# Products of attention probabilities with V: two heads alternating between the column halves of TensorE

## The chip, the cores and the metric

One Trainium2 chip, one core. The metric is the device time of one execution in microseconds (us), as the median of several executions. The profile is one execution, seen by the hardware profiler.

## What is computed

A block of two layers over 512 latent tokens and 256 context tokens, 1024 wide. Each layer runs three token mixers side by side (a recurrence, a full attention, an attention in a window of 128 tokens), merges them with gates, and ends in a mixture of experts. What matters here is the attention. Both kinds have 8 query heads of 64 elements and 2 heads of keys and values, so four query heads share one V. Cut from the reference:

```python
def attend(q, keys, vals):                      # full attention
    qg = q.reshape(q.shape[0], q.shape[1], ATT_KV, group, HEAD_DIM)
    logits = jnp.einsum('bqhgd,bkhd->bhgqk', qg, keys).astype(jnp.float32) * ATTN_SCALE
    p = jax.nn.softmax(logits, axis=-1).astype(vals.dtype)
    o = jnp.einsum('bhgqk,bkhd->bqhgd', p, vals)
```

The windowed kind sees the 256 context keys and up to three tiles of 128 latent keys, and has one more logit per head, a sink. Context queries see context keys alone. All is float32. In the second layer only latent queries are needed.

## The kernel before, in words

Tokens lie in 6 tiles of 128: tiles 0 and 1 are context, 2 to 5 latent. `attention` (L707) makes, for each of the two branches, a unit for keys and values (`attn_kv`, L774) and one unit of queries for each head of keys (`attn_q`, L809), and then calls `attend_unit` (L814) four times per layer: two branches, two heads of keys.

`attend_unit` walks over items: every query tile, and in it four heads. Layer 0 has 6 tiles, so 24 items in a unit; layer 1 has 4 tiles, so 16. Item i passes through stages in successive steps of one loop:

- step i: `attend_qk` (L846) makes the scores S in PSUM (two float32r passes, L876; masks L878), VectorE the row maximum (L883, or L885 and L886), ScalarE the exponential into P with the row sum (L888), VectorE the reciprocal and the scaling of P (L892, L893).
- step i + 2: `attend_t` (L896) transposes P on TensorE in blocks of 128 keys (L904), and ScalarE copies the blocks into a tile PT (L905).
- step i + 3: `attend_pv` (L908) multiplies: for each block of keys one float32 matmul with V (64 columns) as the stationary operand and the block of PT (128 queries) as the moving one (L915). The 64 outputs of a head land in partitions 0 to 63 for an even head and 64 to 127 for an odd one, which are the two halves of the array's columns; heads 0 and 1 share one column block of the accumulator `oT`, heads 2 and 3 the other. After head 3 ScalarE copies the accumulator to `os` (L919) and POOL's queue stores it (L920). `oT` has one buffer.

A head has 2, 4, 5 or 6 blocks of keys. A float32 matmul stands in the trace as two records, each with its own weight load, so a head leaves 4, 8, 10 or 12 records on L915.

After the scores and after the transposes of each step the loop calls `F.fill(fu)`: it issues other work of about `fu` microseconds by the author's own estimate (0.6 to 1.0): gate projections (`gate`, L930; matmuls L503), products of the modulation (`mod`, L277; L286) which go round four quarters of the array's columns, and in some units the projections (L245 to L247) and the key preparation of the next branch. What the fills leave over is issued after the attention. The engines' final order is set when the program is built: a scheduler sorts by priority, which is the order of the code, and by what it estimates to be ready, so neighbours can change places. Semaphores are put in from the use of buffers: a tile of a tag with n buffers waits for the release of the n-th tile before it.

Key preparation (L795 to L806): for each of 6 tiles, ScalarE writes the rounded keys twice into a tile `ks` (L799), VectorE the rests (L801), TensorE transposes four blocks (L805), ScalarE copies them to `kT` (L806). `ks` and PT have two buffers each before the change; P has three.

Of the kernel before, what the change touches and what calls it, by code (L numbers as in the profile page):

```python
# [9 lines left out]
F32 = mybir.dt.float32  # L10
F32R = mybir.dt.float32r
# [12 lines left out]
NT = T // 128  # L24
# [102 lines left out]
class Block:  # L127
# [646 lines left out]
    def attn_kv(self, L, br, p, kv):  # L774
        nc = self.nc
        c0 = COL_ATT[br]
        gk = None
        kv["sink"] = kv["gq"] = None
        if br == 0:
            gq = p.tile([128, 64], F32, name="gq", tag="gq")  # L780
            gk = p.tile([128, 64], F32, name="gk", tag="gk")
            self.bcast(gq, self.I["attn_q_norm_g"][L])
            self.bcast(gk, self.I["attn_k_norm_g"][L])
            nc.vector.tensor_scalar(gq, gq, 0.125, None, op0=OP.mult)
            kv["gq"] = gq
        else:
            sink = p.tile([128, 8], F32, name="sink", tag="sink")
            self.bcast(sink, self.I["swa_sink"][L])
            kv["sink"] = sink
        V = kv["V"] = self.pre.pop(1) if self.pre else p.tile([128, NT, 128], F32, name="aV", tag="aV", bufs=2)  # L790
        w = self.w_split(self.w_load(self.win(L, c0 + 512, 256)))
        yield from self.attn_unit(L, br, p, w, list(range(NT)), 2, gk, 1.0, V)
        raw = self.raw
        kT = kv["kT"] = p.tile([128, 2, 2, T], F32R, name="kT", tag="kT", bufs=2)
        for t in range(NT):  # L795
            ks = p.tile([128, 2, 2, 2, 64], F32R, name="ks", tag="ks", bufs=2)
            hv = raw[:, t, :128].rearrange("p (h d) -> p h d", d=64)
            for d in range(2):
                nc.scalar.activation(ks[:, :, 0, d], hv, AF.Copy)  # L799
            for d in range(2):  # L800
                nc.vector.tensor_tensor(ks[:, :, 1, d], hv, ks.bitcast(F32)[:, :, 0, d], op=OP.subtract)  # L801
            b = self.ps.tile([128, 4, 128], F32R, name="ktp", tag="tp")
            for j in range(2):
                for s in range(2):
                    nc.tensor.transpose(b[:, 2 * j + s, :], ks[:, j, s].rearrange("p a d -> p (a d)"), self.idr[:, :128])  # L805
            nc.scalar.activation(kT[:, :, :, t * 128:(t + 1) * 128].rearrange("p j s t -> p (j s) t"), b, AF.Copy)  # L806
            yield 0.25
# [6 lines left out]
    def attend_unit(self, L, br, p, j, kv, fu):  # L814
        F = self.F
        items = [(t, hh) for t in self.ot for hh in range(4)]
        n = len(items)
        st = {}
        qT = {self.ot[0]: self.attend_q(p, j, self.ot[0], kv)}
        for i in range(n + 3):  # L820
            if i < n:
                t, hh = items[i]
                st[i] = self.attend_qk(L, br, p, j, items[i], kv, qT[t])
                if hh == 1 and i + 3 < n:
                    qT[t + 1] = self.attend_q(p, j, t + 1, kv)
                F.fill(fu)
            if 0 <= i - 2 < n:
                self.attend_t(p, st[i - 2])
                F.fill(fu)
            if 0 <= i - 3 < n:  # L830
                self.attend_pv(L, br, p, j, st.pop(i - 3), kv)

    def attend_q(self, p, j, t, kv):
        nc = self.nc
# [61 lines left out]
    def attend_t(self, p, st):  # L896
        nc = self.nc
        t, hh, kt, P, _ = st
        PT = p.tile([128, NT, 128], F32, name="PT", tag="PT", bufs=2)
        for a in range(0, len(kt), 4):  # L900
            e = min(a + 4, len(kt))
            b = self.ps.tile([128, 4, 128], F32, name="ptp", tag="tp")
            for i in range(a, e):
                nc.tensor.transpose(b[:, i - a, :], P[:, i * 128:(i + 1) * 128], self.ident)  # L904
            nc.scalar.activation(PT[:, a:e], b[:, :e - a], AF.Copy)  # L905
        st[4] = PT

    def attend_pv(self, L, br, p, j, st, kv):  # L908
        nc = self.nc
        t, hh, kt, P, PT = st  # L910
        if hh == 0:
            self.oacc = self.ps.tile([128, 2, 128], F32, name="oT", tag="acc", bufs=1)
        q = slice(64 * (hh % 2), 64 * (hh % 2) + 64)
        for i, k in enumerate(kt):
            nc.tensor.matmul(self.oacc[q, hh // 2, :], kv["V"][:, k, j * 64:(j + 1) * 64], PT[:, i, :],  # L915
                             start=i == 0, stop=i == len(kt) - 1)
        if hh == 3:
            os = self.gp.tile([128, 512], F32, name="os", tag="gt")[:, :256].rearrange("p (a q) -> p a q", a=2)
            nc.scalar.activation(os, self.oacc, AF.Copy)  # L919
            nc.gpsimd.dma_start(self.brD[L][1 + br][:, 2 * j:2 * j + 2, t * 128:(t + 1) * 128], os)  # L920
# [703 lines left out]
```

## Time and profile before

| | |
|---|---|
| median of 3 runs | 3079.65 us (3078.56 to 3084.71) |
| the profiled execution's own time | 3082.0 us |
| its span, first to last instruction | 3080.2 us |
| TensorE busy in the span | 2903.4 us (94%) |
| VectorE, ScalarE, GpSimd busy | 1276.9, 834.4, 369.4 us |
| mean granted TensorE clock | 0.973 of full |

Engines are PE (TensorE matmul), PEld (its weight load, which overlaps PE), DVE (VectorE), ACT (ScalarE), POOL (GpSimd), SP (SyncE). A row of the timeline is: start in us, duration in us, engine, line, operation, what it writes and reads, operand shapes, number of instructions merged into it, and in brackets the idle time before it and what ended that. Matmuls are pipelined: the next one starts before the one before has ended, so the distance of starts tells the rate, not the duration. In the view by windows each row gives a stretch, its length, and then for each engine the busy time and in parentheses the number of instructions that touch the stretch; then the granted clock, the share of DMA time and the GB/s.

### The profile page before, as it was taken

The page shows a single profiled execution, that of the slowest core. Times are in us where ns is not written, and L with a number is a line of the kernel's source. Part 1 is how long each engine was busy: PE and PEld are TensorE (multiplying, and loading weights), DVE is VectorE, ACT ScalarE, POOL GpSimd, SP SyncE. Part 2 cuts the span into 40 slices and gives each one's busy share as a digit, 9 for nine tenths or more (in the row PEclk, how much of TensorE's full clock was granted, in tenths as well). Part 3 has the DMA queues.
Part 4 walks back from the last instruction along what each step waited for, and adds up shares of the span by engine and source line. Part 5 has one row for each costly group of instructions (what it writes and reads, how often), then busy time and mean ns, then how long its engine had stood idle before and what let it go on. Part 6 is the DMA issues. An engine that isn't in the chain of part 4 may idle for free. (4 is left out here: it accounts for less than half of the span.)

```text
span 3080.2 us, 49924 instructions
## 1 busy us (share of the span) xinstructions
PE 2903.4 (94%) x20898; PEld 1989.5 (65%) x20898; DVE 1276.9 (41%) x2693; ACT 834.4 (27%) x1706; POOL 369.4 (12%) x463
## 2 busy tenths in 40 slices
PE   7999999999999969999999799999999988999996
PEld 5999988888899733343333388888888763323321
DVE  5667464454436541221111357666456661211002
ACT  5322244554422210000000143335556320000000
POOL 1001221011111311111100100011000220100000
PEclk9999999999999979999999899999999998999998
DMA  6233333024365568999787612232011668999995
GB/s 234 76 100 121 120 104 104 23 99 137 132 224 192 208 233 337 386 378 354 298 316 294 226 49 72 91 111 68 32 39 61 246 213 359 410 416 413 417 414 204
DMA packets 198652, 640.06 MB, mean 208 GB/s; under 512 B 21584, under 2 KB 87376, under 8 KB 149272
## 3 DMA queue, kind: packets, MB, share of 16 engines
q1 hardware_dynamic: 165960, 552.59, 46.2%
q0 software_dynamic: 31744, 81.58, 8.5%
q8 instruction: 166, 2.72, 0.3%
q10 hardware_dynamic: 720, 2.66, 0.3%
q14 instruction: 62, 0.51, 0.0%
HBM read 600.44 MB, written 57.26 MB: 214 GB/s over the span
## 5 line engine op out<-in xcount | busy, mean ns | idle before, releaser
L503 PE MATMUL ga<-hhi,wsp 128*128 128x384 f32 (+1 forms) x1152 | 356.1, 371 | 1.3 <-DVE mmr L291 0.8
L1537 PE MATMUL gu<-ring,xT 128*32 128x512 f32 x1824 | 332.0, 600 | 8.9 <-DMA ring<-in_w_exp_up 7.0
L1537 PE MATMUL gu<-wspr,xT 128*32 128x512 f32 x1328 | 292.2, 601 | 4.7 <-DMA wspr<-in_w_exp_up 3.6
L1537 PE MATMUL gu<-wraw,xT 128*32 128x512 f32 x1488 | 264.0, 605 | 1.7 <-DMA wraw<-in_w_exp_up 1.6
L1549 PE MATMUL dn<-ring,hT 128*32 128x512 f32 x1128 | 232.6, 595 | 0.0
L239 DVE TENSOR_TENSOR wsp<-wraw,wsp 128x1024 fp32r<-128x1024 f32 x148 | 183.0, 1241 | 112.1 <-ACT wsp L238 104.8
L503 PEld LDWEIGHTS ga<-hhi,wsp 128*128 128x128 f32 x1152 | 209.8, 188 | 18.5 <-issue 2.0
L1537 PEld LDWEIGHTS gu<-ring,xT 128*32 128x32 f32 x1824 | 89.7, 110 | 178.3 <-issue 152.9
L238 ACT ACTIVATE wsp<-wraw 128x1024 fp32r<-128x1024 f32 x148 | 155.6, 1057 | 175.7 <-PE bp L1026 89.9
L915 PE MATMUL oT<-PT,aV 128*64 128x128 f32 x1472 | 193.1, 278 | 1.2 <-ACT PT L905 1.2
L503 PE MATMUL ga<-hlo,wsp 128*128 128x384 f32 (+1 forms) x576 | 190.4, 357 | 0.0
L915 PEld LDWEIGHTS oT<-PT,aV 128*64 128x64 f32 x1472 | 153.5, 136 | 35.1 <-issue 24.6
L1549 PE MATMUL dn<-wspr,hT 128*32 128x512 f32 x688 | 173.8, 596 | 0.0
L1026 PE MATMUL bp<-bhl,wsp 128*128 128x384 f32 (+1 forms) x864 | 167.8, 355 | 1.0 <-ACT bhl L1007 1.0
L1026 PEld LDWEIGHTS bp<-bhl,wsp 128*128 128x128 f32 x864 | 153.6, 188 | 14.8 <-issue 1.2
L1537 PE MATMUL gu<-pf,xT 128*32 128x512 f32 x480 | 155.8, 600 | 1.2 <-DMA pf<-in_w_exp_up 1.2
L1514 POOL DMA_INDIRECT xsD<-yr,ridx x40 | 63.5, 1587 | 760.8 <-DVE yr L1578 527.4
L245 PE MATMUL aacc<-wsp,hhi 128*128 128x256 f32 x512 | 149.8, 292 | 1.2 <-ACT gt L950 1.1
L1537 PEld LDWEIGHTS gu<-wraw,xT 128*32 128x32 f32 x1488 | 68.6, 111 | 123.5 <-issue 113.5
L888 ACT ACTIVATE P<-S,nm 128x768 f32<-128x768 f32 (+3 forms) x160 | 120.0, 750 | 103.2 <-DVE nm L883 54.2
L246 PE MATMUL aacc<-wsp,hhi 128*128 128x256 f32 x512 | 143.8, 281 | 0.0
L1578 DVE SCALAR_TENSOR_TENSOR yr<-dn,wts,G 128x512 f32<-128x512 f32 x48 | 35.6, 749 | 260.3 <-PE dn L1549 232.1
(352 smaller groups left out, 5505.9 us busy)
## 6 DMA issues: line engine op xcount, KB each, us to landing
ring<-in_w_exp_down SPq DMA_DIRECT2D x57, 1024.0 KB, 15.6
ring<-in_w_exp_up SPq DMA_DIRECT2D x51, 1024.0 KB, 13.0
wraw<-in_w_mod SPq DMA_DIRECT2D x46, 1024.0 KB, 5.4
wraw<-in_w_in SPq DMA_DIRECT2D x42, 1024.0 KB, 4.9
wraw<-in_w_exp_gate SPq DMA_DIRECT2D x40, 1024.0 KB, 8.9
ring<-in_w_exp_gate SPq DMA_DIRECT2D x39, 1024.0 KB, 16.5
wspr<-in_w_exp_gate SPq DMA_DIRECT2D x34, 1024.0 KB, 18.3
wraw<-in_w_exp_up SPq DMA_DIRECT2D x34, 1024.0 KB, 9.9
```

Source lines behind the costliest of these rows:

```text
L238: self.nc.scalar.activation(hv, src, AF.Copy)
L239: (self.nc.gpsimd if len(parts) in slow else self.nc.vector).tensor_tensor(lv, src, hv.bitcast(F32), op=OP.subtract)
L245: mm(out, l[0], r[0], start=start, stop=False)
L246: mm(out, l[0], r[1], start=False, stop=False)
L503: mm(o, w(k)[wi][:, fs], self.h[hi_][:, k, a:a + s], start=k == 0 and wi == 0 and hi_ == 0, stop=k == 7 and wi == 1)
L888: nc.scalar.activation(P[:, :nk], S[:, :nk], AF.Exp, bias=nm[:, 0:1], accum_out=nm[:, 2:3])
L915: nc.tensor.matmul(self.oacc[q, hh // 2, :], kv["V"][:, k, j * 64:(j + 1) * 64], PT[:, i, :], start=i == 0, stop=i == len(kt) - 1)
L1026: nc.tensor.matmul(o[:, c, :step], w(k)[wi][:, fs], b[:, 4 * hi + k, c * step:(c + 1) * step], start=k == 0 and wi == 0 and hi == 0, stop= ...
L1514: self.nc.gpsimd.indirect_dma_start(out=self.xsD[L][:, :], out_offset=bass.IndirectOffsetOnAxis(ap=idx, axis=0), in_=y[:, :], in_offset=No ...
L1537: self.nc.tensor.matmul(o[c], xT[n][:, 4 * h + k, c], w(g, k), start=h + k == 0, stop=h * k == 3)
L1549: self.nc.tensor.matmul(b[c], h[:, k, c], w[k // 2](g, k % 2)[:, js], start=k == 0, stop=k == 3)
L1578: V.scalar_tensor_tensor(y[:, js], b, wt, G, op0=OP.mult, op1=OP.mult)
```

## The change

The products of an even and the following odd head are issued together, in every second step: for each block of keys first the even head's matmul, then the odd head's. A step with even i takes items i − 4 and i − 3; the transposes keep their step. Since two finished PT tiles wait while a third is written, PT has three buffers; `ks` has one. The accumulator is copied and stored after the pair that begins with head 2.

```diff
-            ks = p.tile([128, 2, 2, 2, 64], F32R, name="ks", tag="ks", bufs=2)
+            ks = p.tile([128, 2, 2, 2, 64], F32R, name="ks", tag="ks", bufs=1)
...
-            if 0 <= i - 3 < n:
-                self.attend_pv(L, br, p, j, st.pop(i - 3), kv)
+            if 0 <= i - 3 < n and i % 2 == 0:
+                self.attend_pv(L, br, p, j, (st.pop(i - 4), st.pop(i - 3)), kv)
...
-        PT = p.tile([128, NT, 128], F32, name="PT", tag="PT", bufs=2)
+        PT = p.tile([128, NT, 128], F32, name="PT", tag="PT", bufs=3)
...
-    def attend_pv(self, L, br, p, j, st, kv):
-        nc = self.nc
-        t, hh, kt, P, PT = st
+    def attend_pv(self, L, br, p, j, pair, kv):
+        nc = self.nc
+        t, hh, kt = pair[0][:3]
         if hh == 0:
             self.oacc = self.ps.tile([128, 2, 128], F32, name="oT", tag="acc", bufs=1)
-        q = slice(64 * (hh % 2), 64 * (hh % 2) + 64)
         for i, k in enumerate(kt):
-            nc.tensor.matmul(self.oacc[q, hh // 2, :], kv["V"][:, k, j * 64:(j + 1) * 64], PT[:, i, :],
-                             start=i == 0, stop=i == len(kt) - 1)
-        if hh == 3:
+            for a, st in enumerate(pair):
+                nc.tensor.matmul(self.oacc[64 * a:64 * a + 64, hh // 2, :], kv["V"][:, k, j * 64:(j + 1) * 64], st[4][:, i, :],
+                                 start=i == 0, stop=i == len(kt) - 1)
+        if hh == 2:
```

## Rows read from the trace of the kernel before

**Rows 1.** The profile page, busy us and share of the span by engine.
```profile
PE 2903.4 (94%) x20898; PEld 1989.5 (65%) x20898; DVE 1276.9 (41%) x2693; ACT 834.4 (27%) x1706; POOL 369.4 (12%) x463
```

**Rows 2.** View by windows, all engines, the attention stretches of layers 0 and 1.
```profile
437.00:846.00 409.00, 406.63 (x3447) 355.32 (x3449) 201.23 (x498) 204.68 (x539) 56.06 (x89) 1.00 0.31 103
2137.00:2400.00 263.00, 259.69 (x1863) 222.44 (x1864) 141.11 (x317) 153.05 (x377) 16.95 (x26) 0.99 0.13 45
```

**Rows 3.** The same windows, L915 alone.
```profile
437.00:846.00 409.00, 106.61 (x800) 83.18 (x800) 1.00 0.31 103
2137.00:2400.00 263.00, 86.46 (x672) 70.35 (x672) 0.99 0.13 45
```

**Rows 4.** Waits of TensorE, 2137 to 2400 us: us in total, times, longest.
```profile
PE ptp L904 <- DVE P L893: 2.5, 1, 2.5
...
PE oT L915 <- ACT PT L905: 0.7, 1, 0.7
```

**Rows 5.** All matmul records of L915: count, duration in ns min/median/max.
```profile
L915 PE MATMUL oT<-PT,aV x1472: 272/273/324, 440.2 to 2396.9; 128*64 128x128 f32 x184
```

**Rows 6.** Timeline of TensorE around heads of 12 and of 8 records.
```profile
632.75 0.34 PE L503 MATMUL ga<-hlo,wsp 128*128 128x384 f32 x1
632.92 0.34 PE L503 MATMUL ga<-hhi,wsp 128*128 128x384 f32 x1
633.19 1.52 PE L915 MATMUL oT<-PT,aV 128*64 128x128 f32 x12
634.65 0.98 PE L876 MATMUL S<-kT,qT 128*128 128x512 f32 x4
635.47 0.34 PE L503 MATMUL ga<-hhi,wsp 128*128 128x384 f32 x1
...
681.23 1.09 PE L915 MATMUL oT<-PT,aV 128*64 128x128 f32 x8
682.25 0.73 PE L876 MATMUL S<-kT,qT 128*128 128x512 f32 x2
```

**Rows 7.** Timeline of TensorE, four score matmuls with no product ahead.
```profile
2130.26 0.86 PE L876 MATMUL S<-kT,qT 128*128 128x512 f32 x4
2130.95 0.40 PE L503 MATMUL ga<-hhi,wsp 128*128 128x512 f32 x1
```

**Rows 8.** Timeline of TensorE: two heads back to back, and the modulation product.
```profile
534.21 2.45 PE L915 MATMUL oT<-PT,aV 128*64 128x128 f32 x24
536.59 0.45 PE L503 MATMUL ga<-hhi,wsp 128*128 128x384 f32 x1
...
616.24 1.96 PE L286 MATMUL macc<-wraw,cs 128*32 128x128 f32 x64
618.12 1.52 PE L915 MATMUL oT<-PT,aV 128*64 128x128 f32 x12
```

**Rows 9.** View by windows, L915 alone, two stretches inside the burst at 534.21.
```profile
534.88:535.21 0.33, 0.33 (x6) 0.33 (x6) 1.00 0.00 0
535.21:535.54 0.33, 0.33 (x9) 0.33 (x8) 1.00 0.00 0
```

**Rows 10.** View by windows, all engines and then L915 alone, two stretches of layer 1.
```profile
2360.00:2400.00 40.00, 38.22 (x285) 31.54 (x284) 24.72 (x68) 29.34 (x75) 4.88 (x8) 1.00 0.16 51
2140.00:2160.00 20.00, 20.00 (x146) 16.76 (x144) 12.37 (x21) 12.83 (x30) 1.33 (x2) 0.98 0.22 73
...
2360.00:2400.00 40.00, 18.38 (x136) 14.33 (x136) 1.00 0.16 51
2140.00:2160.00 20.00, 9.36 (x72) 7.67 (x72) 0.98 0.22 73
```

**Rows 11.** Timeline of key preparation in layer 1: copies, transposes, and the copy to kT.
```profile
2100.46 0.51 ACT L799 ACTIVATE ks<-araw 128x128 fp32r<-128x128 f32 x2 [1.83 <-DVE araw L771]
...
2100.81 0.54 PE L805 MATMUL ktp<-idr,ks 128*128 128x128 f32 x4 [0.78 <-DVE ks L801]
...
2101.30 0.60 ACT L806 ACTIVATE kT<-ktp 128x512 fp32r<-128x512 f32 x1 [0.33 <-PE ktp L805]
```

## The prediction, made before the change was run

> **What bounds the kernel now.** I read the totals by engine first: TensorE is busy 94% of the span, no other engine half of it [rows 1]. An average over the whole program proves little for one stage, so next come the stretches that hold the products with V, one per layer: 409 and 263 us long. In both TensorE is busy 99%, at a granted clock of 1.00 and 0.99, that is at 2.4 GHz; ScalarE is busy 50 and 58%, VectorE 49 and 54%, and the DMA engines 31 and 13% [rows 2]. The products themselves (L915) hold TensorE for 106.6 and 86.5 us of that [rows 3]. Then the waits, in the second stretch, where ScalarE's share is the higher: TensorE's longest is 2.5 us, once, and on the copy of PT it waits 0.7 us [rows 4]. So here TensorE is the path, the softmax of a head runs beside it, and time taken from TensorE comes off the end, until ScalarE or VectorE is late in its turn.
>
> **What a product costs now.** A float32 matmul leaves two records, so the 736 matmuls of L915 are 1472 records [rows 5]. Measured from the first record to the first of the next group, a head of 12 records takes 634.65 − 633.19 = 1.46 us, one of 8 takes 682.25 − 681.23 = 1.02 [rows 6]: 4 records make 0.44, so 0.11 us per record and 0.14 us beside. Two more costs lie outside. Gate matmuls follow each other at 0.17 us, but the product starts 0.27 us after the last of them: 0.10 to enter [rows 6]. The four score matmuls after it take 0.82 us [rows 6], against 0.69 where no product stands ahead [rows 7]: 0.12 to leave. So a head costs 0.11 us per record and 0.36 us fixed.
>
> There are 160 heads (96 in layer 0, 64 in layer 1). 1472 × 0.11 + 160 × 0.36 = 161.9 + 57.6 = 219.5 us. In 8 places, one at the end of each unit, two heads already stand back to back as one burst; for 24 records that takes 2.38 us instead of 2 × 1.46, and saves 0.22 for the second entry and exit: 0.76 each at most, 6 in all. Before: **about 214 us**.
>
> **Do the halves overlap?** These same bursts answer it, since the second head lies in the other column half. One after the other, 24 records would take 0.14 + 24 × 0.11 = 2.78 us; they take 536.59 − 534.21 = 2.38 [rows 8]. The count by windows shows where: 6 records touch a window of 0.33 us while one half works, 9 where the first head ends and the second begins [rows 9]. A record lasts 0.273 us [rows 5], so 6 is one start per 0.10 us and 9 one per 0.067, and that window holds the edges of the overlap too. The modulation product (L286) goes round four quarters of the columns with rows of the same 128 elements: 64 records in 618.12 − 616.24 = 1.88 us, 16 rounds of 0.117 [rows 8]. A round of four takes what one record takes alone. I therefore take 0.11 us for a round of two.
>
> The trace bounds the price of a round between 0.11 (the four quarters) and 0.22 (two records in one half); it is nearest to the first, whose loop has the same form. The first record of a half lasts 0.324 us instead of 0.273, its weight load being exposed [rows 5]; each of the 1472 weight loads shown is otherwise hidden under the previous record, or the heads could not run at 0.11. The Trainium skill, "TensorE: Matmul & The Clock Gate", section "Part 3: Packing small matmuls — row/col tiling", says a weight load overlaps matmuls in flight only when its row group differs; here both halves use all 128 rows, so by that rule the sum would be a loss of 50 us, not a gain (the last rival). The trace speaks against it for loads that follow in one half.
>
> **The sum.** A pair now is one burst: per record pair 0.11 us, 0.36 us fixed, 0.05 for the second half's own first load. 736 × 0.11 + 80 × 0.41 = 81 + 33 = 114 us. TensorE is relieved of 214 − 114 = **100 us**. No matmul, copy, exponential or DMA is added or removed: same 40 accumulators, same 40 stores on POOL's queue, issued at the second pair instead of the fourth head. The next tile's first product now comes two steps after the copy of the accumulator, not one, so that wait only loosens. SP's loads are not moved past anything. The even head's product waits up to a step longer for its partner's PT; what queues behind it on TensorE are scores and filler of the next step, and the partner's PT was copied a full step earlier (scores, transposes and two fills between). The third PT buffer is what keeps the copy of the following head from waiting for the pair. All that costs nothing while a step holds filler: filler and transposes cover the partner's copy, and without them TensorE would wait for one copy of PT, as it did for the 0.7 us above.
>
> **Where a part stays behind.** The products lie densest in 2140 to 2160 and in 2360 to 2400 us, 9.4 of 20 and 18.4 of 40 us [rows 10]. In the latter 136 records would give back 136 × 100/1472 = 9.2 us, leaving 30.8 us for 29.3 us of ScalarE work [rows 10]. ScalarE is nowhere in these rows busier than 73%, and the chain from scores over maximum, exponential, scaling, transposes to PT runs through it; at 82%, my choice between 73 and 100, the stretch would need 35.8 us: 5 us of the 9.2 are lost. The other stretch gives back 4.9 of 20 us, against 12.8 of ScalarE [rows 10]: 15.1 left, 15.6 needed, 0.5 lost. What is late next there is the scaled P for the transposes, and then PT. Lost: **5.5 us**; bounds 0 and half of the 100 (first rival).
>
> **One ks buffer.** Key preparation runs 24 times (two branches, two layers, six tiles). With one buffer ScalarE's copies of tile t + 1 wait for the transposes of tile t; behind them in ScalarE's queue stand PT copies and exponentials in the second branch. The chain of a tile is a copy pair 0.51 us, the last subtraction about 0.3 after it (my estimate from the start of the transposes), transposes 0.54 [rows 11], 1.35 us, against 0.51 + 0.60 = 1.11 for ScalarE alone now [rows 11]. Difference 0.24 × 24 = 6 us if nothing covers it, 32 us if the chain is wholly exposed, 0 if filler or the next projection (which already stands between these transposes) covers it. I take **2 us**.
>
> Sum: 100 − 5.5 − 2 = 92.5 us less. Against the profiled execution's 3082.0 us that is 2989.5; this execution lies 2.35 above the median of the runs, 3079.65, so on the median's scale **2987 us**.
>
> **The rivals.**
> *The softmax chain takes over* (22%). If the steps become so short that TensorE waits for P or PT everywhere, not only where filler is thin, about half is kept: 50 us, 3030. For it: ScalarE waits for scores or transposes and TensorE's order is fixed, so each delay is TensorE's too. Against: 358 us of ScalarE in 672 [rows 2] would be 62% of the 572 left, and scores stand two steps ahead of their transposes.
> *More than counted* (8%): nothing is lost and short waits vanish: 2966 to 2975.
> *The change does not do what it says* (5%): the order in the built program keeps the two heads apart, or the halves take turns. Then only the merging is won: 80 × 0.36 − 6 = 23 us, less 2: about 3059. Against: the four quarters of L286 are issued in the same way.
> *Slower* (3%): at every change of half the weight load is exposed, as it is now only for a half's first record (0.324 − 0.273 = 0.05). If no load hides behind the other half's matmul, each record costs 0.16 us: 1472 × 0.16 + 80 × 0.36 = 264 us against 214, 50 us slower, 3130. It turns into a loss once a record costs more than (214 − 29)/1472 = 0.126. Its place is each switch inside a pair; the overlapped stretch of 0.33 us with 9 records speaks against it. The rule of the Trainium skill named above would have this outcome.
>
> **How the numbers follow.** The forecast (60%) spans 2972 to 3005: the fixed price may be 0.1 us off per pair, the two losses between 0 and 20. The range adds most of the case above and most of the softmax case: **2966 to 3030**. A measurement of this kernel tells about 0.2% (6 us) from no change. The first four cases are faster, 95%; the slower rival 3%; 2% stay for an unforeseen order of the program that eats the gain: same.
>
> **What would show it.** Right: the records of L915 stay 1472, in some 80 bursts of 24, 20, 16 or 8; a burst of 24 takes about 1.5 us to the next group; L915 holds TensorE for about half of 193 us; both attention stretches are shorter by some 54 and 38 us at unchanged clock, and the stages around them keep their lengths. Wrong: bursts of 24 that take over 2.4 us (halves in turn), or waits of TensorE for P, PT or ks that add up to tens of us, or a stretch outside attention that grows by what attention gave.

## The result, and the profile after

The changed kernel takes 3008.9 us (median of 4 runs, 3005.3 to 3011.2) against 3080.9 for the kernel before (4 runs): ratio 0.9771, 95% interval 0.9758 to 0.9783, so 72 us faster. A second set of runs gave 0.9767 (0.9752 to 0.9782). The forecast was 2987, in a range of 2966 to 3030: sign and mechanism hold, the gain is 78% of the 92.5 us forecast.

The totals of the profile page answer to [rows 1]:

```profile
span 3009.0 us, 49938 instructions
...
PE 2822.9 (94%) x20898; PEld 1924.1 (64%) x20898; DVE 1270.4 (42%) x2693; ACT 835.1 (28%) x1706; POOL 370.3 (12%) x463
```

To say where the time went I cut both programs alike: from the first score matmul of a layer to the first matmul of the merge behind its attention. View by windows, first the kernel before, then the changed one (layer 0, layer 1):

```profile
436.80:887.50 450.70, 448.33 (x3700) 396.83 (x3700) 210.72 (x507) 214.71 (x554) 65.53 (x106) 1.00 0.34 118
2125.90:2398.20 272.30, 266.88 (x1901) 228.43 (x1900) 148.16 (x332) 157.52 (x385) 18.55 (x28) 0.99 0.13 45
```

```profile
437.80:850.10 412.30, 403.38 (x3699) 361.53 (x3699) 205.30 (x507) 216.24 (x554) 66.36 (x106) 0.99 0.38 129
2085.70:2325.00 239.30, 229.93 (x1903) 195.54 (x1901) 146.52 (x327) 156.47 (x384) 18.54 (x28) 1.00 0.14 50
```

The two stretches are shorter by 38.4 and 33.0 us, 71.4 together; the profiled executions differ by 3082.0 − 3010.8 = 71.2. Outside attention nothing is gained or lost on balance: the part ahead of the first stretch, the part between the two and the part behind them differ by +1.0, −2.8 and +2.0 us. In the shorter stretches ScalarE is busy as long as before (372 and 373 us), VectorE 7 us less. The forecast had 54 and 38 us, so layer 0 falls short by 16 and layer 1 by 5. TensorE's idle time, length less busy, rose from 2.4 + 5.4 = 7.8 us to 8.9 + 9.4 = 18.3.

The same windows, L915 alone, answer to [rows 3]: 108.8 us in all, where it was 193.1.

```profile
437.80:850.10 412.30, 59.90 (x800) 44.73 (x800) 0.99 0.38 129
2085.70:2325.00 239.30, 48.89 (x672) 37.89 (x672) 1.00 0.14 50
```

And the pair itself, in the timeline of TensorE, against [rows 6] and [rows 8]:

```profile
473.15 0.34 PE L503 MATMUL ga<-hhi,wsp 128*128 128x384 f32 x1
473.42 1.53 PE L915 MATMUL oT<-PT,aV 128*64 128x128 f32 x24
474.88 0.98 PE L876 MATMUL S<-kT,qT 128*128 128x512 f32 x4
475.69 0.46 PE L842 MATMUL qtp<-idr,qs 128*128 128x128 f32 x4
```

24 records of two heads take 474.88 − 473.42 = 1.46 us to the next group: exactly what 12 records of one head took. The two halves run side by side: 12 rounds of two take what 12 single records took. Entering (0.27 after a gate matmul) and leaving (0.81 for the scores) cost what they did.

But not every pair is one burst:

```profile
505.95 0.43 PE L915 MATMUL oT<-PT,aV 128*64 128x128 f32 x2
506.31 0.45 PE L503 MATMUL ga<-hhi,wsp 128*128 128x384 f32 x1
...
507.67 1.52 PE L915 MATMUL oT<-PT,aV 128*64 128x128 f32 x22
509.13 0.96 PE L876 MATMUL S<-kT,qT 128*128 128x512 f32 x4
```

Here the even head's first product, whose PT is ready early, stands alone ahead of the rest; the 22 records behind it take 1.46 us all the same, so its 0.36 us and an entry and exit are lost. Counted along the timeline, L915 forms 104 groups instead of 80 (163 before).

TensorE's waits in layer 0's stretch, before and after (us in total, times, longest):

```profile
PE S L876 <- ACT P L888: 1.0, 1, 1.0
PE ptp L904 <- DVE P L893: 0.5, 1, 0.5
PE oT L915 <- ACT PT L905: 0.4, 1, 0.4
```

```profile
PE S L876 <- ACT P L888: 2.3, 1, 2.3
PE ktp L805 <- ACT ks L799: 1.5, 2, 1.1
PE ptp L904 <- ACT PT L905: 1.4, 1, 1.4
PE ga L503 <- ACT gt L950: 1.2, 2, 0.8
PE aacc L246 <- DVE wsp L239: 0.7, 1, 0.7
```

These are all waits over 0.15 us before but one of 0.3, and the five largest after. No wait dominates. Most lead to ScalarE, and several to work that is no softmax: keys, gates, weights.

### The profile page after: what moved, and what is told of

Same layout as the page of the kernel before. It is cut to its first block, busy times and chain, and to the rows that moved or that the text cites. A ratio compares the mean times of both kernels' runs of the same rounds, so it can differ in the third digit from the quotient of the medians.

```text
span 3009.0 us, 49938 instructions
## 1 busy us (share of the span) xinstructions
PE 2822.9 (94%) x20898; PEld 1924.1 (64%) x20898; DVE 1270.4 (42%) x2693; ACT 835.1 (28%) x1706; POOL 370.3 (12%) x463
## 5 line engine op out<-in xcount | busy, mean ns | idle before, releaser
L1559 DVE TENSOR_TENSOR hs<-hs,gu 128x512 f32<-128x512 f32 x40 | 27.5, 687 | 277.8 <-PE gu L1537 270.9
L247 PE MATMUL aacc<-wsp,hlo 128*128 128x256 f32 x512 | 143.9, 282 | 0.0
```

The costliest lines, as they stand in the source:

```text
L247: mm(out, l[1], r[0], start=False, stop=stop)
```

## The experiments

The theory to be tested: alternation halves the products' time on TensorE (A), and the shortfall of 20 us is partly products that are split off and partly waits which the shorter steps expose. Rivals: the gain is the merging of bursts and not the overlap; the shortfall is the single ks buffer; it is the softmax chain. In each expectation below, theory A and the rivals are that run's own. Idle times are length less busy, in stretches cut as above.

### Pairs without alternation

```diff
-        for i, k in enumerate(kt):
-            for a, st in enumerate(pair):
+        for a, st in enumerate(pair):
+            for i, k in enumerate(kt):
```

> The changed kernel, but the pair's products run through all blocks of the even head and then all of the odd head; steps, buffers and everything else as changed. Theory A (the gain is the overlap of the two column halves inside a round): a burst of 24 records takes about 2.4 us to the next group instead of 1.46, because only the end of one head overlaps the start of the other; 80 bursts then lose most of 80 x 0.6 to 0.9, so this kernel is 40 to 60 us slower than the changed one, about 3050 us, ratio to before 0.985 to 0.992. Theory B (the gain is the merging of two entries into the 64-column form into one, and the calmer order of every second step): it stays within 8 us of the changed kernel, ratio 0.976 to 0.980.

Measured: 3051.1 us, ratio 0.9902 (0.9886 to 0.9917). Timeline of TensorE around a pair:

```profile
472.12 2.46 PE L915 MATMUL oT<-PT,aV 128*64 128x128 f32 x24
474.50 0.97 PE L876 MATMUL S<-kT,qT 128*128 128x512 f32 x4
```

The same 24 records take 2.38 us instead of 1.46. Theory A holds: alternation is needed for more than half of the gain. Of the 72 us some 33 come from pairing (fewer groups, and the end of one head over the start of the other) and some 40 from alternation. The stretches, all engines:

```profile
436.80:869.90 433.10, 427.08 (x3701) 385.94 (x3700) 205.69 (x507) 216.61 (x554) 65.89 (x106) 1.00 0.36 122
2105.20:2363.90 258.70, 252.03 (x1903) 218.56 (x1901) 146.78 (x327) 156.12 (x384) 18.49 (x28) 1.00 0.14 46
```

Idle is 6.0 + 6.7 = 12.7 us, between the 7.8 before and the 18.3 after: the less TensorE has to do, the more it waits.

### One ks buffer, in the kernel before

```diff
-            ks = p.tile([128, 2, 2, 2, 64], F32R, name="ks", tag="ks", bufs=2)
+            ks = p.tile([128, 2, 2, 2, 64], F32R, name="ks", tag="ks", bufs=1)
```

> The kernel before with one ks buffer instead of two and nothing else. Theory A (the single buffer explains a few us of the shortfall against the forecast): 2 to 6 us slower than before, ratio 1.0007 to 1.002, and waits on ks of 2 to 6 us more in the trace. Rival (it explains the whole shortfall of about 20 us): ratio 1.005 or more. Rival (fully covered): ratio within 0.0005 of 1.

Measured: ratio 1.0003 (0.9994 to 1.0012): no measurable cost, against a forecast of 2 us; the interval allows up to 4. Alone it does not explain the shortfall. In layer 0, where the second branch's keys are prepared between the heads, 17 us of the kernel before, then of this one:

```profile
563.00:580.00 17.00, 16.58 (x129) 14.44 (x128) 12.99 (x29) 12.88 (x34) 0.72 (x1) 1.00 0.21 71
```

```profile
563.00:580.00 17.00, 14.84 (x109) 12.56 (x107) 11.99 (x28) 11.45 (x30) 0.72 (x1) 1.00 0.21 71
```

TensorE idles 2.2 us there instead of 0.4; the clock stays at 2.4 GHz.

### The odd head first

```diff
-            for a, st in enumerate(pair):
+            for a, st in ((1, pair[1]), (0, pair[0])):
```

> The changed kernel with the odd head ahead of the even one in each block of keys. In the changed kernel 104 bursts stand where 80 pairs were meant: often the even head's first product, whose PT is ready early, is placed alone ahead of the rest. With the odd head first, whose PT is ready last, the built order has 94 bursts. Theory A (each needless burst costs its entry, exit and tail, 0.36 us): 10 x 0.36, about 4 us faster than the changed kernel, ratio to before about 0.976. Rival (the shortfall is waits, not splits): within 3 us of the changed kernel, ratio 0.977, with waits of TensorE in the attention stretches as large as in the changed kernel.

Measured: 3008.6 us, ratio 0.9755 (0.9742 to 0.9769); the changed kernel lies at 0.9771 with an interval that overlaps. The groups fell to 94. L915 alone, then all engines:

```profile
437.50:848.20 410.70, 56.25 (x800) 42.62 (x800) 0.99 0.38 129
2084.70:2322.20 237.50, 45.08 (x672) 35.91 (x672) 1.00 0.15 52
```

```profile
437.50:848.20 410.70, 400.51 (x3699) 359.59 (x3698) 204.97 (x507) 215.65 (x554) 66.40 (x106) 0.99 0.38 129
2084.70:2322.20 237.50, 226.62 (x1902) 192.96 (x1902) 147.09 (x332) 156.65 (x385) 18.54 (x28) 1.00 0.15 52
```

The products take 101.3 us, 7.5 less than in the changed kernel, but idle grew to 10.2 + 10.9 = 21.1, by 2.8, and the stretches together are only 3.4 us shorter. The medians do not decide it; what theory A saved on TensorE was at least partly turned into waiting.

### The products ahead of the transposes

```diff
+            if 0 <= i - 3 < n and i % 2 == 0:
+                self.attend_pv(L, br, p, j, (st.pop(i - 4), st.pop(i - 3)), kv)
             if 0 <= i - 2 < n:
                 self.attend_t(p, st[i - 2])
                 F.fill(fu)
-            if 0 <= i - 3 < n and i % 2 == 0:
-                self.attend_pv(L, br, p, j, (st.pop(i - 4), st.pop(i - 3)), kv)
...
-        PT = p.tile([128, NT, 128], F32, name="PT", tag="PT", bufs=3)
+        PT = p.tile([128, NT, 128], F32, name="PT", tag="PT", bufs=2)
```

and ks with two buffers again.

> The changed kernel with the pair's products ahead of the step's transposes instead of behind them; then two PT buffers and two ks buffers are enough, so no buffer changes against before. Theory A (the third PT buffer isn't needed for the gain, and the ks buffer costs a few us): as fast as the changed kernel or up to 6 us faster, ratio 0.975 to 0.977. Rival (the odd head's PT is copied too late when only scores and one fill stand between its transposes and its product): TensorE waits for PT at many of the 80 pairs, 10 us or more in total, ratio 0.980 or more.

Measured: 3002.5 us, ratio 0.9743 (0.9730 to 0.9757), some 8 us better than the changed kernel, a little more than the 6 that theory A allowed. TensorE's waits for PT come to 3.2 us in its two stretches, not 10 or more. The third PT buffer isn't needed if the products that free the buffers come first; the next run confirms that.

### The same with one ks buffer

```diff
-            ks = p.tile([128, 2, 2, 2, 64], F32R, name="ks", tag="ks", bufs=2)
+            ks = p.tile([128, 2, 2, 2, 64], F32R, name="ks", tag="ks", bufs=1)
```

> Products ahead of the transposes and two PT buffers as in the earlier variant, but one ks buffer as in the changed kernel; it differs from that variant in the ks buffer alone. Theory A (the single ks buffer costs a few us once the steps are short, though it cost nothing measurable in the kernel before): 3 to 6 us slower than that variant, so about as fast as the changed kernel, ratio 0.9755 to 0.977, with waits on ks back in layer 0's attention. Rival (the order of products and transposes gave the gain): ratio 0.974 to 0.975.

Measured: 3011.8 us, ratio 0.9770 (0.9754 to 0.9785), no better than the changed kernel. So by the medians the ks buffer is what the variant above won, 0.0027 or 8 us. Every run with one buffer (3005.3 to 3014.2) is slower than every run with two (3001.7 to 3004.9), but the intervals just overlap: by their edges −1 to 17 us. In the profiled executions the two attention stretches differ by 6.5 us, 4.6 of them in layer 0. The stretch of key preparation in layer 0, with two ks buffers, then with one:

```profile
549.00:566.00 17.00, 16.62 (x142) 14.55 (x141) 12.73 (x30) 14.15 (x35) 0.72 (x1) 1.00 0.21 72
```

```profile
555.00:572.00 17.00, 13.91 (x93) 11.58 (x92) 11.43 (x29) 10.90 (x32) 0.72 (x1) 0.90 0.21 70
```

With one buffer TensorE idles 3.1 us of these 17, and the granted clock is 0.90 on average: 1.2 GHz for 3.4 us from 568.2 us on, behind most of the waits, at a cost of some 1.7 (estimate: half of 3.4). With two it idles 0.4 and keeps 2.4 GHz. The changed kernel has the same fall, at 567.7 us. A fall at this place stands in all seven profiled executions with one ks buffer and alternating pairs, and in neither of the two with two buffers and such pairs, nor in the one without alternation.

The other fall in layer 0 does not need the single ks buffer: it stands behind the wait for S at the start of the first unit, at 455.1 us in the changed kernel and at 452.6 with products ahead and two ks buffers. In the changed kernel 32 records of the modulation take 1.94 us in it, against 1.08 ahead of it:

```profile
451.10 1.08 PE L286 MATMUL macc<-wraw,cs 128*32 128x128 f32 x32
454.48 1.16 PE L876 MATMUL S<-kT,qT 128*128 128x512 f32 x4 [2.30 <-ACT P L888]
455.57 1.94 PE L286 MATMUL macc<-wraw,cs 128*32 128x128 f32 x32
```

### Without the division by the row sum

```diff
-        nc.vector.reciprocal(nm[:, 2:3], nm[:, 2:3])
-        nc.vector.tensor_scalar(P[:, :nk], P[:, :nk], nm[:, 2:3], None, op0=OP.mult)
```

In the changed kernel, which here leaves out the division:

> The changed kernel without the reciprocal and the scaling of P by the row sum (that division is left out of the computation): 160 reciprocals and 160 scalings less on VectorE, and the chain from scores to transposes shorter by some 0.8 us per head. Theory A (what the change did not bring is TensorE running into the chain of the softmax, because the steps became shorter): TensorE's idle time in the two attention stretches falls from 18 us to under 10, and the kernel is 8 to 15 us faster than the changed one, ratio to before about 0.973. Rival (the waits sit behind other work in the queues of ScalarE and VectorE, or come with the order fixed at build): within 4 us of the changed kernel, idle time 14 us or more.

And as a control in the kernel before:

> The control: the kernel before without the reciprocal and the scaling (the same division left out). There TensorE idles 8 us in the two stretches, so both theories expect within 4 us of before, ratio 0.9985 to 1.001. If it gains as much as the run above gains against the changed kernel, the chain was no nearer to the path after the change than before it.

Measured: 3002.2 us, ratio 0.9751 (0.9736 to 0.9766), and for the control 3076.4, ratio 0.9991 (0.9981 to 1.0000). All engines, changed kernel without the division:

```profile
435.60:843.80 408.20, 402.31 (x3700) 360.43 (x3699) 148.65 (x315) 214.96 (x554) 65.14 (x106) 1.00 0.38 130
2075.90:2312.20 236.30, 227.39 (x1902) 194.37 (x1901) 105.93 (x204) 156.07 (x385) 18.47 (x28) 1.00 0.15 52
```

VectorE lost 97 of 352 us there, and TensorE still idles 5.9 + 8.9 = 14.8 us instead of 18.3. The gain is 6.7 us against 2.4 or so in the control. Neither prediction fits whole; the idle time fits the rival. By the medians the length of the chain is worth some 4 us of the shortfall; the intervals overlap those of the two whole kernels, so zero is not excluded. In the trace the wait for S at the start of the first unit is 1.3 us instead of 2.3, and the clock does not fall behind it.

### More filler in layer 0

```diff
-    AF = ({1: 0.8, 2: 1.0, 4: 0.8, 5: 0.8}, {1: 0.6, 2: 1.0, 4: 0.6, 5: 0.6})
+    AF = ({1: 1.0, 2: 1.25, 4: 1.0, 5: 1.0}, {1: 0.6, 2: 1.0, 4: 0.6, 5: 0.6})
```

> The changed kernel with a quarter more filler after each scores and each transposes in layer 0 (0.8 to 1.0 and 1.0 to 1.25), layer 1 as it was. No work is added, filler only comes earlier and less is left for the end of the attention. Theory A (shorter steps leave too little cover for the softmax): layer 0's TensorE idle time falls from 8.9 us to under 6, and the kernel is 2 to 5 us faster than the changed one. Rival (the waits do not depend on the cover): within 2 us, idle unchanged.

Measured: 3012.6 us, ratio 0.9785 (0.9771 to 0.9798). Layer 0, all engines:

```profile
436.50:849.10 412.60, 403.30 (x3700) 364.16 (x3698) 204.58 (x506) 216.24 (x555) 63.43 (x103) 0.99 0.35 117
```

Idle 9.3 us, as without. Theory A falls here: a quarter more filler does not help. In layer 0 of the changed kernel 2.3 us of the 8.9 stand in the one wait at the start of the first unit and 2.8 at key preparation; the rest is scattered. At the start of the unit VectorE is working through the rotation of `araw` (L769 to L771) and takes the row maximum (L883), which the release of S waits for, only behind it:

```profile
452.21 0.68 DVE L770 TENSOR_TENSOR araw<-araw,artmp 128x512 f32<-128x512 f32 x1
452.81 0.68 DVE L771 TENSOR_TENSOR araw<-araw,artmp 128x512 f32<-128x512 f32 x1
453.41 0.74 DVE L883 TENSOR_REDUCE nm<-S 128x1 f32<-128x256 f32 x2
```

### Both orders together

Products ahead, two PT and two ks buffers, and the odd head first (both diffs above).

> Both variants together: products ahead of the transposes, two PT and two ks buffers, and the odd head first in each block. The built order has 92 bursts. Theory A (each needless burst costs about 0.36 us beside what the single variants showed): 3 to 6 us faster than the variant with products ahead alone, ratio to before 0.972 to 0.974. Rival (waiting for the odd head's PT takes it back): no faster than that variant, ratio 0.974 to 0.977.

Measured: 2998.2 us, ratio 0.9733 (0.9720 to 0.9747): about 10 us faster than the changed kernel, and the best measured. The step from the variant with products ahead alone (0.9743) is within the intervals.

```profile
434.90:840.80 405.90, 397.52 (x3700) 358.34 (x3699) 207.82 (x507) 216.53 (x554) 65.81 (x106) 1.00 0.38 131
2076.00:2313.20 237.20, 225.71 (x1902) 193.83 (x1901) 146.76 (x332) 158.06 (x385) 18.46 (x28) 0.99 0.15 51
```

The stretches come to 643.1 us against 651.6 of the changed kernel, with 8.4 + 11.5 = 19.9 us idle.

### The changed kernel again, and every round twice

> The changed kernel itself, beside the two runs below on the same chip: ratio to before 0.976 to 0.978, as measured first.

Measured: 3008.3 us, ratio 0.9767 (0.9752 to 0.9782).

```diff
         for i, k in enumerate(kt):
-            for a, st in enumerate(pair):
-                nc.tensor.matmul(..., start=i == 0, stop=i == len(kt) - 1)
+            for r in range(2):
+                for a, st in enumerate(pair):
+                    nc.tensor.matmul(..., start=i + r == 0, stop=r == 1 and i == len(kt) - 1)
```

> The changed kernel with every round issued twice (the products with V come out doubled): 736 more rounds of two records. It prices a round, and tells whether attention is still bound by TensorE. At 0.11 us for a round, 80 us more of TensorE's time. Theory A (TensorE is still the path, and the longer steps hide part of the waits that the change exposed): 62 to 80 us slower than the changed kernel, TensorE's idle time in the two stretches back under 14 us. Rival (the softmax now sets the pace): under 50 us slower. Rival (a round costs more than one record alone): over 85 us.

Measured: 3082.3 us, ratio 1.0008 (0.9998 to 1.0017), 74 us above the changed kernel in the same set: twice the products, alternating, take what the products took once in the kernel before. The new loop moves the products to L916. Timeline of TensorE, then all engines:

```profile
474.70 2.84 PE L916 MATMUL oT<-PT,aV 128*64 128x128 f32 x48
477.47 0.97 PE L876 MATMUL S<-kT,qT 128*128 128x512 f32 x4
```

```profile
437.30:895.50 458.20, 450.59 (x4500) 407.62 (x4499) 206.77 (x507) 216.34 (x554) 66.20 (x106) 0.99 0.34 116
2128.60:2401.00 272.40, 265.04 (x2575) 231.61 (x2573) 149.06 (x332) 156.38 (x385) 18.59 (x28) 1.00 0.13 45
```

12 more rounds in a burst cost 2.77 − 1.46 = 1.31 us, 0.109 each, so 736 rounds are 80 us; 74 reached the end, and idle fell to 7.6 + 7.4 = 15.0, a little over the 14 expected. Theory A holds in the time: attention is still bound by TensorE.

## Why the prediction was right, and where a term was off

**What bounds the kernel** was right: all of the gain lies in the two stretches, and TensorE's time still passes to the end at 74 of 80 us.

**The price of a round** was right: 0.11 us for two records in different halves, measured as 1.46 us for 24 records and 0.109 us per doubled round. The slower rival and the rule of the Trainium skill behind it ("TensorE: Matmul & The Clock Gate", "Part 3: Packing small matmuls — row/col tiling") do not hold for column halves: had each weight load waited for the other half, a burst of 24 would have taken 24 × 0.16 = 3.8 us by the rival's price. The sentence that I cited was too narrow to go by alone: the same section of the Trainium skill lists a speedup of 2.38× for three tiles of 32 columns. The traces agree that column tiles run side by side: two halves reach 2.0× (24 records in the 1.46 us of 12). That the change does not do what it says is refuted too: without alternation the pair takes 2.38 us.

**The sum, "A pair now is one burst"**, was mis-sized. From the first record of each group to the next instruction, L915 took 182.8 us in 163 groups before and 104.9 in 104 groups after; with 0.22 us for entering and leaving each, that is 219 us before, where I had 214, and 128 after, where I had 114. TensorE was relieved of 77.9 + 59 × 0.22 = 91 us, not 100. Whole pairs (16 each of 8, 16 and 20 records at 0.59, 1.02 and 1.24 us, 32 of 24 at 1.46) would take 92.4, and 83 groups less would save 18: 109. The prediction named the built order as a risk, but only for a pair kept apart, not for its first product pulled ahead.

**"Where a part stays behind"** and **"One ks buffer"** together were 7.5 us; 91 − 71 = 20 were lost. I had looked for late work in the second stretch alone, because ScalarE's share was higher there; some 13 of the 20 were lost in layer 0. The trace shows 10.5 us more idle time in the two stretches. The clock, which I had expected unchanged, fell to 1.2 GHz twice in layer 0, 3.4 us each, where it had not before; but layer 1's stretch held one such fall before (at 2137.4 us) and only the last 1.0 us of one after, so the falls cost some 2.2 us more on balance (an estimate: half of the time at the lower level). The remaining 7 do not show as idle time. An estimate from the distances of starts on TensorE (each against the 15th percentile for its two kinds of records over seven of the traces, products left out) finds delays over 0.15 us of 10 us before and 27 after, so most of the 20 are delays, part of them hidden where records overlap in the trace.

By cause: the ks buffer some 8 us, not 2, by the medians of the two variants that differ in it alone, with a wide interval. I had bounded it by the chain of one tile and not thought of the clock behind the wait. The softmax chain is worth some 4 us by the run without the division, near my 5.5 but not clear of zero. The place that I had named at the end of layer 1 did lose: from the same score matmul to the merge, before and then after,

```profile
2361.70:2398.20 36.50, 34.75 (x267) 29.22 (x266) 22.44 (x63) 26.19 (x69) 3.08 (x5) 1.00 0.15 48
2291.60:2325.00 33.40, 28.72 (x269) 23.36 (x267) 22.96 (x65) 25.94 (x70) 3.12 (x5) 1.00 0.15 53
```

3.1 us were kept of the 8.7 that 128 records should have given back by my sum. ScalarE is busy 78% there after the change; my 82% was a choice without a row, so that it came close is partly luck. The first rival (half of the gain lost) did not come. The other 8 us or so seem to be waits behind other work in the queues of ScalarE and VectorE, as in the row of L883 above; no run here took that work away, so which of it costs what stays open.

## What to carry to other kernels

Two products that each fill half of the array's columns cost the price of one if they alternate matmul by matmul; look in the trace for any place where two halves already meet and measure the overlap there. When the bounding engine is relieved by an eighth in a stretch, as here, expect part of it back as waits: in this kernel 71 of 91 us reached the end, and 74 of 80 on the way back. Look first at buffers that the change took away to make room. Put the instruction that frees a buffer ahead of the one that needs it, before adding a buffer.

## What was not expected of the hardware

A single ks buffer cost nothing measurable in the kernel before and about 8 us with the pairs in place: with the shorter steps TensorE idled 3.1 of 17 us at key preparation, and the granted clock fell to its lower level (1.2 GHz) for 3.4 us behind the waits. A wait that grew from 1.0 to 2.3 us, at the start of the first unit, was followed by such a fall too: 32 modulation records took 1.94 us behind the wait at 454.48 us, 1.08 ahead of it.
